# Dividing the exponentials before the transposes, instead of the outputs after the value product

## The chip, the cores and the metric

The kernel runs on one core of a Trainium2 chip. The metric is the device time of one execution in microseconds, as the median of several runs. TensorE (PE) multiplies matrices and also does the transposes; VectorE (DVE), ScalarE (ACT) and GpSimd (POOL) work element by element; SyncE (SP) issues the loads.

## The reference, cut to what matters

Two networks follow each other on 256 tokens of width 1024. The first is a mixer with a mixture of experts. The second has two layers; each normalizes, projects to queries, keys and values, attends, gates the attention's output with silu(z), and projects back. The change lies in the attention of these two layers alone. What it has to compute is, for each head of width 64 with 512 keys (256 of a context, 256 latent):

```
s = q @ k.T * scale (+ mask or position bias)     # layer 0, heads 0-7: one more logit, the sink, in the sum
p = softmax(s, axis=-1)
o = (p @ v) * silu(z)
```

Layer 0 has eight heads with grouped keys and a sink and eight latent-attention heads; layer 1 has sixteen neighbourhood heads with a bias. All is float32.

## The kernel before, in words

The weights stream from memory. Each piece is split into a high part (ACT, tile `whi`) and a rest (`wlo`, DVE, every fourth piece POOL), and each projection is three matmuls per block (`gmm`, line 314). That is most of PE's work.

The attention of a layer is cut into 16 units (`unit`, line 2219): a unit is one pair of heads `c` and one block of 128 queries `i`. `x0_units` makes the units of layer 0 (the first eight with a sink, `sink_softmax`; the last eight with `plain_softmax`), `x1_units` those of layer 1. A unit goes in three parts:

- Scores: for both heads s, scores into a PSUM bank of their own (tag "t", six banks); DVE adds mask or bias and takes the row maximum (`snm`); ACT takes the exponentials into `P` (tile `sP`, three buffers) and their row sums into `sm` (tile `ssm`). DVE turns `sm` into its reciprocal (line 2233), POOL spreads that over 64 columns a head (`rs`, tile `rsb`, line 2234).
- Transposes: `P`, not yet divided, is transposed on PE in eight 128x128 pieces (line 2240 by way of line 433) and evicted to `PT`, the first head by ACT, the second by DVE.
- Values: PE turns `rs` (line 2243) into the first 128 columns of a bank, and multiplies `PT` with the values (line 2246) into the next 128. The first write into the output tile `oz` (tile `xoz`) is ACT's copy of the turned reciprocals, and DVE then multiplies by the values' product; where the gate is there already, DVE multiplies twice instead.

The order on PE is written out in the program: `drive` (line 143) runs all streams (three lanes of units, the projection, the closing steps, small turns) on a clock of its own. A stream that yields `(cost, late)` moves that clock by its cost and may go on only `late` after it; of those that are due, the first in the list goes, and the projection, always due, fills the rest in steps (about 655 clock units for the six matmuls of a step of 256 columns). A unit starts at least `UNIT_GAP` = 3300 after the one before; its transposes follow `UNIT_P` after the scores, its values `UNIT_T` = 1600 after the transposes:

```
yield (900, UNIT_P)      # after the scores
yield (900, UNIT_T)      # after the transposes
yield 1200               # after the values
```

PE, and every other engine, executes its instructions in order. On the other engines a scheduler of the framework sets the order at build time. The context's attention of the first layers (lines 1751 and 1792) already divides its exponentials by `scaled` (line 1861), with 256 keys.

Of the kernel before, what the change touches and what calls it, by code (L numbers as in the profile page):

```python
# [12 lines left out]
OP = mybir.AluOpType  # L13
# [24 lines left out]
POOL_A = 4  # L38
POOL_C = 4
UNIT_GAP = 3300  # L40
UNIT_P = 3000
UNIT_T = 1600
UNIT_Q = 5000
LANES = 3
# [225 lines left out]
class Net:  # L270
# [1948 lines left out]
    def unit(self, c, i, needs, scores, soft, vals):  # L2219

        nc, Y, pm = self.nc, self.Y, self.pm
        mm = nc.tensor.matmul
        yield from self.wait(*needs)
        yield (0, max(0.0, max(self.done.at[n] for n in needs) + UNIT_Q - CLOCK[0]))
        yield ("unit", UNIT_GAP)
        rows = []
        for s in range(2):
            b = self.bank(pm, "t", 6)
            scores(b, s)
            rows.append(b)  # L2230
        P, sm = soft(rows)
        rs = self.t(Y, [128, 128], "rsb", 2)
        nc.vector.reciprocal(sm, sm)
        nc.gpsimd.tensor_copy(rs.rearrange("p (s d) -> p s d", s=2), sm[:, :, None].to_broadcast([128, 2, 64]))
        self.done.add("s%d%d" % (c, i))
        yield (900, UNIT_P)
        PT = self.t(Y, [128, 2, 4, 128], "PT", 2)
        for s in range(2):
            b = self.transposes([(128 * k, P[:, s, 128 * k:128 * k + 128]) for k in range(4)], pm, "t", 6)
            (self.copy if s else self.act)(PT[:, s], b.rearrange("p (k q) -> p k q", k=4))  # L2240
        yield (900, UNIT_T)
        b = self.bank(pm, "t", 6)
        nc.tensor.transpose(b[:, 0:128], rs, self.ident)
        for k in range(4):
            for s in range(2):
                mm(b[64 * s:64 * s + 64, 128:256], vals(k, s), PT[:, s, k], start=False, stop=k == 3,  # L2246
                   skip_group_check=True)
        o = self.oz[:, c, 128 * i:128 * i + 128]
        if "g%d" % (c // 2) in self.done:
            self.tt(o, b[:, 0:128], o, OP.mult)  # L2250
            self.tt(o, b[:, 128:256], o, OP.mult)
        else:
            self.act(o, b[:, 0:128])
            self.tt(o, b[:, 128:256], o, OP.mult)
        self.done.add("o%d%d" % (c, i))
        yield 1200

# [298 lines left out]
```

## Time and profile before

| | us |
|---|---|
| median of 3 runs | 1212.33 (1212.28 to 1212.49) |
| the profiled execution | 1215.19 |
| its span, first to last instruction | 1213.4 |
| busy in the span: PE / DVE / ACT / POOL | 1096.5 / 561.3 / 452.6 / 192.1 |

The profile is of one execution. Busy shares are means over stages with different limits, so a stage is read by itself: the units of layer 0 run from about 895 to 990 us, those of layer 1 from about 1064 to 1170 us. A row of the windows view gives the stretch, its length, and for each engine its busy us and instructions (PEld is the loading of weights on PE), then the granted clock as a share of full speed and the share and GB/s of the DMA engines. In a row of instructions, "tile<-inputs" names what is written and read, and a bracket at its end is the idle time of the engine before it and what ended that.

### The profile page before, as it was taken

The numbers are of one execution on the slowest core, as the hardware profiler recorded it, in microseconds if no ns is written. First come the engines' busy times: TensorE is split into PE (matmuls) and PEld (weight loads), VectorE is DVE, ScalarE is ACT, GpSimd is POOL, SyncE is SP. The second block draws the span as 40 slices with busy tenths as digits, with TensorE's granted clock in tenths as the row PEclk, the third lists the DMA queues.
The fourth block names the chain that finished last, engine by engine and source line by source line (L and its number), as shares of the span: only waits on it lengthen the run. The fifth ranks groups of instructions, "written<-read, shape, count | busy, mean of one in ns | idle before, by whom it ended". The sixth has DMA issues, their size and how long they took to land. (4 is left out here: it accounts for less than half of the span.)

```text
span 1213.4 us, 19686 instructions
## 1 busy us (share of the span) xinstructions
PE 1096.5 (90%) x7695; PEld 759.6 (63%) x7695; DVE 561.3 (46%) x1393; ACT 452.6 (37%) x1107; POOL 192.1 (16%) x210
## 2 busy tenths in 40 slices
PE   5999999998989998788889899957989996999996
PEld 5878777785335664333444265312877786999996
DVE  5366773454131211432311210105797677677776
ACT  4634564541012101222310200004576554676663
POOL 6134102211000000000000000001311143335231
PEclk8999999997999999999999899998999998899999
DMA  7898659972999999999999999997435275355331
GB/s 252 294 303 269 209 168 322 344 286 96 395 407 407 400 403 405 404 405 408 404 402 406 405 405 405 405 400 262 150 105 157 70 145 157 112 142 124 122 111 60
DMA packets 171321, 337.62 MB, mean 278 GB/s; under 512 B 20053, under 2 KB 92826, under 8 KB 171226
## 3 DMA queue, kind: packets, MB, share of 16 engines
q1 hardware_dynamic: 169706, 333.78, 76.5%
q0 software_dynamic: 1104, 2.45, 0.7%
q8 instruction: 62, 1.02, 0.3%
q14 instruction: 33, 0.27, 0.1%
q10 hardware_dynamic: 416, 0.10, 0.1%
HBM read 331.58 MB, written 4.73 MB: 277 GB/s over the span
## 5 line engine op out<-in xcount | busy, mean ns | idle before, releaser
L317 ACT ACTIVATE whi<-wst 128x512 fp32r<-128x512 f32 (+4 forms) x240 | 149.2, 629 | 107.5 <-PE m L314 97.4
L217 DVE TENSOR_TENSOR wlo<-wst,whi 128x512 fp32r<-128x512 f32 (+4 forms) x180 | 137.8, 772 | 82.5 <-ACT whi L317 81.4
L217 POOL TENSOR_TENSOR wlo<-wst,whi 128x512 fp32r<-128x512 f32 (+4 forms) x60 | 80.2, 1337 | 484.6 <-ACT whi L317 407.0
L1390 PE MATMUL g<-we,xg 128*32 128x512 f32 x632 | 127.3, 612 | 11.4 <-DMA we<-in_w_up_dram 9.2
L314 PE MATMUL m<-whi,uhi 128*128 128x256 f32 (+2 forms) x368 | 108.7, 295 | 2.8 <-ACT uhi L317 1.9
L314 PE MATMUL m<-wlo,uhi 128*128 128x256 f32 (+2 forms) x368 | 104.8, 285 | 1.8 <-POOL wlo L217 1.8
L314 PE MATMUL m<-whi,ulo 128*128 128x256 f32 (+2 forms) x368 | 104.7, 285 | 0.0
L314 PE MATMUL s<-cuT,wst 128*128 128x256 f32 (+1 forms) x368 | 85.8, 385 | 0.0
L314 PEld LDWEIGHTS s<-cuT,wst 128*128 128x128 f32 (+1 forms) x368 | 64.7, 183 | 27.6 <-issue 17.1
L314 PEld LDWEIGHTS m<-whi,uhi 128*128 128x128 f32 x368 | 70.5, 192 | 13.0 <-issue 5.8
L314 PE MATMUL m<-xhi,whi 128*128 128x256 f32 x256 | 75.6, 295 | 0.0
L314 PE MATMUL m<-xhi,wlo 128*128 128x256 f32 x256 | 72.4, 283 | 0.0
L314 PE MATMUL m<-xlo,whi 128*128 128x256 f32 x256 | 72.3, 283 | 0.0
L314 PEld LDWEIGHTS m<-wlo,uhi 128*128 128x128 f32 x368 | 70.4, 191 | 2.1 <-POOL wlo L217 2.0
L314 PEld LDWEIGHTS m<-whi,ulo 128*128 128x128 f32 x368 | 70.3, 191 | 0.3 <-POOL ulo L503 0.3
L1421 PE MATMUL d<-we,hT 128*32 128x512 f32 x336 | 59.2, 616 | 6.8 <-DMA we<-in_w_down_dram 6.8
L1390 PEld LDWEIGHTS g<-we,xg 128*32 128x32 f32 x632 | 25.9, 110 | 59.7 <-issue 35.2
L314 PE MATMUL s<-wst,cuT 128*128 128x512 f32 (+1 forms) x160 | 53.7, 480 | 0.0
L314 PEld LDWEIGHTS m<-xhi,whi 128*128 128x128 f32 x256 | 48.9, 191 | 2.7 <-issue 2.5
L314 PEld LDWEIGHTS m<-xlo,whi 128*128 128x128 f32 x256 | 48.9, 191 | 0.7 <-issue 0.5
L314 PEld LDWEIGHTS m<-xhi,wlo 128*128 128x128 f32 x256 | 48.9, 191 | 0.0
L314 PE MATMUL m<-whi,xhi 128*128 128x256 f32 (+2 forms) x144 | 43.2, 300 | 5.2 <-ACT xhi L317 5.0
(611 smaller groups left out, 2303.2 us busy)
## 6 DMA issues: line engine op xcount, KB each, us to landing
we<-in_w_down_dram SPq DMA_DIRECT2D x48, 1024.0 KB
we<-in_w_up_dram SPq DMA_DIRECT2D x40, 1024.0 KB
we<-in_w_gate_dram SPq DMA_DIRECT2D x39, 1024.0 KB
we<-in_ada_w_dram SPq DMA_DIRECT2D x24, 1024.0 KB
wst<-in_c_in_w_dram SPq DMA_DIRECT2D x24, 1024.0 KB
wst<-in_w_in_dram SPq DMA_DIRECT2D x17, 1024.0 KB
wst<-in_ab_in_w_dram SPq DMA_DIRECT2D x16, 1024.0 KB
vc<-in_w_gate_dram SPq DMA_DIRECT2D x12, 1024.0 KB
```

The source lines that it names most:

```text
L217: (net.nc.gpsimd if pool else net.nc.vector).tensor_tensor(b, src, a, OP.subtract)
L314: mm(out, l, r, start=first and i == 0, stop=last and i == len(ps) - 1, skip_group_check=True)
L317: return self.nc.scalar.activation(out, in_, f, **kw)
L1390: nc.tensor.matmul(b[32 * e:32 * e + 32, :], xg[:, 2 * j + r, 32 * e:32 * e + 32], v[e // 2][:, e % 2, 512 * r:512 * r + 512], start=j == ...
L1421: nc.tensor.matmul(ds[hf][32 * e:32 * e + 32, :], hT[:, k, 32 * e:32 * e + 32], v[e // 2][:, e % 2, 512 * hf:512 * hf + 512], start=k == 0 ...
```

## The change

`P` is divided where it lies, by DVE, one instruction a head, ahead of the transposes; the spreading of the reciprocals, their transpose on PE and the second multiplication into `oz` go; the values' product starts its bank by itself. `UNIT_P` goes from 3000 to 4000.

```diff
-UNIT_P = 3000
+UNIT_P = 4000
...
         P, sm = soft(rows)
-        rs = self.t(Y, [128, 128], "rsb", 2)
         nc.vector.reciprocal(sm, sm)
-        nc.gpsimd.tensor_copy(rs.rearrange("p (s d) -> p s d", s=2), sm[:, :, None].to_broadcast([128, 2, 64]))
+        for s in range(2):
+            self.ts(P[:, s], P[:, s], sm[:, s:s + 1])
...
         b = self.bank(pm, "t", 6)
-        nc.tensor.transpose(b[:, 0:128], rs, self.ident)
         for k in range(4):
             for s in range(2):
-                mm(b[64 * s:64 * s + 64, 128:256], vals(k, s), PT[:, s, k], start=False, stop=k == 3,
+                mm(b[64 * s:64 * s + 64, 0:128], vals(k, s), PT[:, s, k], start=k == 0, stop=k == 3,
                    skip_group_check=True)
         o = self.oz[:, c, 128 * i:128 * i + 128]
         if "g%d" % (c // 2) in self.done:
             self.tt(o, b[:, 0:128], o, OP.mult)
-            self.tt(o, b[:, 128:256], o, OP.mult)
         else:
             self.act(o, b[:, 0:128])
-            self.tt(o, b[:, 128:256], o, OP.mult)
```

`self.ts(out, a, s)` is DVE's tensor_scalar: each row of `a` times that row's scalar `s`.

## Rows read from the trace of the kernel before

**Rows 1.** Windows: busy us of PE, PEld, DVE, ACT, POOL; clock; DMA.
```profile
895.00:915.00 20.00, 17.68 (x130) 14.91 (x129) 19.57 (x87) 14.07 (x39) 2.77 (x4) 1.00 0.50 143
945.00:990.00 45.00, 45.00 (x369) 36.39 (x367) 30.80 (x60) 25.82 (x62) 10.03 (x14) 1.00 0.35 95
1064.00:1080.00 16.00, 16.00 (x141) 14.31 (x141) 13.56 (x31) 12.73 (x30) 5.88 (x7) 1.00 0.49 148
```

**Rows 2.** PE's waits, 1064 to 1170 us: us in total, times, longest.
```profile
PE t L2246 <- DVE PT L331: 1.0, 2, 0.6
```

**Rows 3.** The chain of waits: start us, us, engine, line; here only PE.
```profile
1072.59 0.11 PE t L2243
1072.69 1.02 PE t L2246 x16
...
1074.74 0.72 PE m L314 x6
```

**Rows 4.** Groups of what goes: min/median/max ns, or busy us, mean ns.
```profile
L2243 PE MATMUL t<-tab,rsb x32: 270/272/328, 906.2 to 1167.7; 128*128 128x128 f32 x32
L2234 POOL COPY rsb<-ssm x32: 287/294/611, 902.7 to 1164.4; 128x128 f32<-128x128 f32 x32
...
L320 DVE TENSOR_TENSOR xoz<-t,xoz 128x128 f32<-128x128 f32 x32 | 9.2, 287 | 7.3 <-ACT xoz L317 7.0
```

**Rows 5.** The timeline of PE around one such transpose: start us, us.
```profile
1072.42 0.27 PE L2243 MATMUL t<-tab,rsb 128*128 128x128 f32 x1
1072.62 0.66 PE L2246 MATMUL t<-PT,vc 128*64 128x128 f32 x8
```

**Rows 6.** Tensor_scalar on DVE: the group of line 327, then timeline rows.
```profile
L327 DVE TENSOR_SCALAR sP<-sP,ssm x32: 344/351/354, 475.9 to 605.5; 128x256 f32<-128x256 f32 x32
...
475.75 0.17 DVE L1862 RECIPROCAL ssm<-ssm 128x2 f32<-128x2 f32 x1
475.95 0.62 DVE L327 TENSOR_SCALAR sP<-sP,ssm 128x256 f32<-128x256 f32 x2
...
685.94 1.41 DVE L327 TENSOR_SCALAR cxa<-cuT,rcy 128x1024 f32<-128x1024 f32 x2
```

**Rows 7.** The timeline at the third unit of each four in layer 1.
```profile
1074.96 0.28 DVE L320 TENSOR_TENSOR xoz<-t,xoz 128x128 f32<-128x128 f32 x1
1075.16 0.68 DVE L331 COPY PT<-t 128x512 f32<-128x512 f32 x1
...
1076.22 0.49 PE L433 MATMUL t<-tab,sP 128*128 128x128 f32 x3
1076.31 0.17 DVE L2233 RECIPROCAL ssm<-ssm 128x2 f32<-128x2 f32 x1 [0.47 <-ACT sP L317]
...
1099.28 1.04 PE L433 MATMUL t<-tab,sP 128*128 128x128 f32 x8
1099.65 0.17 DVE L2233 RECIPROCAL ssm<-ssm 128x2 f32<-128x2 f32 x1 [0.49 <-ACT sP L317]
...
1130.77 0.93 PE L433 MATMUL t<-tab,sP 128*128 128x128 f32 x7
1131.08 0.17 DVE L2233 RECIPROCAL ssm<-ssm 128x2 f32<-128x2 f32 x1 [0.42 <-ACT sP L317]
...
1160.29 0.93 PE L433 MATMUL t<-tab,sP 128*128 128x128 f32 x7
1160.38 0.17 DVE L2233 RECIPROCAL ssm<-ssm 128x2 f32<-128x2 f32 x1 [0.42 <-ACT sP L317]
```

**Rows 8.** The timeline at a unit of layer 0 with a sink.
```profile
915.71 1.32 PE L433 MATMUL t<-tab,sP 128*128 128x128 f32 x8 [0.98 <-ACT sP L317]
...
916.45 0.16 DVE L320 TENSOR_TENSOR ssm<-ssm,ssk 128x2 f32<-128x2 f32 x1 [0.34 <-ACT ssk L317]
```

**Rows 9.** The timeline of DVE and POOL, 874 to 877 us.
```profile
874.28 2.33 DVE L327 TENSOR_SCALAR xqb<-xqb,rs4y 128x384 f32<-128x384 f32 x4
...
875.20 1.26 POOL L217 TENSOR_TENSOR wlo<-wst,whi 128x512 fp32r<-128x512 f32 x1 [3.50 <-ACT whi L317]
```

## The prediction

> **What bounds the kernel now.** Begin with the windows of the two stretches in which units run, since the shares of the whole span mix them with other stages. From 945 us on PE is busy for every microsecond of the stretch, and again in layer 1; the granted clock is 1.00 there [rows 1]. PE's waits say the same: in the 106 us of layer 1's units it loses 1.0 us, on an eviction by DVE [rows 2]. The head of layer 0 is different: between 895 and 915 us DVE is busy for 19.57 of 20 us and PE for 17.68 [rows 1]. So PE's work is the time of most units, DVE's at the head of layer 0, and DVE stands close behind PE where layer 1's units are dense (13.56 of 16 us).
>
> Then look at where a unit's reciprocal lies against its transposes, in the timeline. PE begins the transposes as soon as the exponentials are there; in the third unit of each four of layer 1 the reciprocal starts only after that, by 0.09, 0.37, 0.31 and 0.09 us [rows 7]. Now that costs nothing, for nobody needs the reciprocal until the values' product. The change puts it, and two more instructions, ahead of the transposes.
>
> **What goes.** On PE 32 transposes of the spread reciprocals. In the chain of waits, which follows end to end, one takes 0.11 us [rows 3], so 32 x 0.11 = 3.5 us. From its start to the start of the product behind it are 0.20 us [rows 5], but that holds the product's own beginning; 32 x 0.20 = 6.4 us is the upper end. I take 3.5, since PE is the bound nearly wherever they stand. On DVE one multiplication a unit, 0.287 us long [rows 4], with 0.20 us from its start to the next instruction's [rows 7]. POOL's spreading (0.294 us, [rows 4]) gates the product alone and is no PE wait in layer 1 [rows 2]: nothing for the path.
>
> **What comes.** Two tensor_scalars of 128x512 a unit. No row has that width. One of 256 columns takes 0.351 us; two take 0.62, so the second starts 0.27 after the first; two of 1024 columns take 1.41 [rows 6]. A pair of 512 by proportion: 0.62 + (1.41 - 0.62)/3 = 0.88, one 0.48, start to start 0.40. The bounds for a unit are 0.62 and 1.41; I take 0.88, with 0.80 of DVE's time, net 0.60 after the multiplication that goes. From the start of the reciprocal to a divided first head are 0.20 [rows 6] + 0.48 = 0.68 us, some 0.70 with the hop to PE. The second head (0.20 + 0.88) is needed four transposes later and isn't what decides.
>
> **What moves.** `UNIT_P` puts the transposes 1000 clock units later. What that is in PE work has to be followed through the planner, for the projection comes in steps of about 655. At 3000, the first unit of four (scores at clock 0, cost 900) is due at 3900, behind the second unit's scores, which end at 4424: it goes at once. At 4000 it is due at 4900: one step goes ahead, then it. The other three also gain one step, not one and a half. A step is six matmuls, 0.72 us [rows 3]. The transposes take their evictions, the product and the write into `oz` along; no load is issued in these parts. The exponentials' three buffers serve three lanes with one unit each, so the longer hold delays no one. Steps that come forward by 0.72 us need their weights that much earlier; PE has no wait on a split in these stretches now [rows 2], so I take nothing for it, with 1 us for both layers as the upper end.
>
> **The sum for layer 1.** Take the third unit of the first four [rows 7]. PE would begin its transposes at 1076.22 + 0.72 - 0.11 (one reciprocals' transpose less ahead of it) = 1076.83. The reciprocal comes later, because DVE is in order and full: the two units ahead put 2 x 0.80 in front of it, one multiplication of 0.20 goes, and 0.47 us of idle time ahead of it take up a part: 0.93 later, at 1077.24. Divided at 1077.24 + 0.70 = 1077.94: PE waits 1.11 us. In the same way 0.37 + 0.91 + 0.70 - 0.61 = 1.37, then 0.31 + 0.98 + 0.09 = 1.38 and 0.09 + 0.98 + 0.09 = 1.16 for the other three [rows 7]; together 5.0 us. A wait of PE moves the units behind it along too, so one for each four is counted, at its third unit. Behind the waiting transposes PE's queue holds projection steps, the product of the unit before and the scores of the next, all of them on the path. The lower end is 0 (DVE's order, set anew, has the divisions in time); the upper, with pairs of 1.41 us, about 3 x 0.5 us more for each four, is 11.
>
> **The sum for layer 0.** At the head DVE is full and PE waits for it [rows 1]. Three units have their reciprocal before 915 us: 3 x 0.60 = 1.8 us. A sink's unit needs one more hop: the sum with the sink is ready at 916.61, so the divided head could be there at about 917.3, while its transposes begin at 915.71 [rows 8]: 1.6 us late, less a step of 0.72, 0.9. The later units with a sink have projection work beside them: 0.3 for all. Together 3.0; 0 is the lower end (work put off past 915 us), 5 the upper, with 0.9 for two more. From 945 to 990 us DVE is busy for 30.8 of 45 us [rows 1] and takes up 8 x 0.60 = 4.8 more: nothing.
>
> Sum: -3.5 + 5.0 + 3.0 = +4.5 us. On the profiled execution, 1215.19 us (span 1213.4 and 1.8 around it), that is 1219.7; the median of the runs is 2.9 below that execution, so 1216.8.
>
> **A rule against the change.** Four tensor_scalars (two of 384, two of 256 columns) took 2.33 us, where the pairs above would give about 1.3, and a POOL split of 1.26 us began among them [rows 9]. The Trainium skill (SBUF — State Buffer, "Who interferes with whom") says that VectorE in a two-port mode, which a float32 tensor_scalar within SBUF can enter, and GpSimd take turns on one port pair, the second waiting for the whole instruction of the first; by that rule, the trace agrees, these divisions would queue behind POOL's splits. As a mechanism of these rows: in layer 1's first four POOL is busy for 5.88 of 16 us, 4.7 without the four spreadings, so a tensor_scalar meets one with a chance of 0.29 and waits half of 1.26 us, 0.18 in the mean; five of them ahead of the third unit's transposes make 0.9 us for each four, 3.7 in layer 1.
>
> **Rivals.**
> *The cover is enough* (chance 0.20): the divisions are in time, the saving is left: 1215.19 - 3.5 - 2.9 = 1208.8. It ends on the other side, by one mechanism: at the third unit of each four, DVE has the reciprocal 1.1 to 1.4 us earlier than I reckon, because its order, set anew, puts weight splits behind the divisions. For it: the idle time ahead of each reciprocal in rows 7. Against: DVE's 13.56 of 16 us [rows 1], and that full DVE at 895 to 915 us would have to take 1.8 us more for nothing.
> *Gain and wait cancel* (0.25): only the head of layer 0 pays in full, and a tenth of layer 1's waits come: -3.5 + 3.0 + 0.5 = 0, 1212.3. For it: layer 1's DVE has 2.4 us of idle time in those 16 us [rows 1], and the head of layer 0 none.
> *Divisions behind POOL* (0.13): the mechanism of rows 9 on top of the forecast, +8.2 us: 1220.5. It decides once a third of the divisions meet POOL. Against: POOL loses 32 instructions, and some divisions will be first.
> *Forecast* (0.42): 1216.8, by itself 1214.8 to 1219.
>
> **The numbers.** About 0.2% (2.4 us) is what a measurement of this kernel tells from no change. Slower by more: forecast and POOL, 0.42 + 0.13 = 0.55; within: 0.25; faster: 0.20. The range goes from the full saving, 1208.8, past the POOL case to 1221.0; below it lies a saving of 0.20 a transpose, above it pairs of 1.41 us, together about one in ten, and as much again for what I haven't seen.
>
> **What would show it.** Right: PE's waits in layer 1 name the tensor_scalar (line 327) ahead of transposes (line 433), about 1.2 us at each four, mostly at third units; DVE in 1064 to 1080 goes from 13.6 to over 15 us; between 895 and 915 us PE's busy time falls. The removed transposes shorten PE's work by 3.5 us in all. Wrong: no such waits in layer 1 (then the time is at or under 1212), transposes moved by other than one step, a tensor_scalar far from 0.48 us, or waits in other stretches.

## The result, and the profile after

| | us |
|---|---|
| before, median of 5 runs | 1212.49 (1212.28 to 1215.32) |
| after, median of 5 runs | 1230.71 (1228.41 to 1235.15) |
| ratio after/before, 95% interval | 1.0143 (1.0127 to 1.0160) |
| the profiled execution of after, and its span | 1235.15, 1233.4 |

The change made the kernel slower by 1.43%, some 17 us. The sign was forecast; the size was not. The forecast was +4.5 us, and 1230.71 lies above the range.

Where the time went is found by cutting both executions at the same work, not at the same microsecond: from the first scores of layer 0 to its first out-projection matmul (the units of layer 0), from there to the first scores of layer 1 (call it the seam), from there to the first out-projection matmul of layer 1 (its units). The windows view gives one row for each of the three; its columns are those of [rows 1]. First the kernel before:

```profile
895.60:990.08 94.48, 91.42 (x729) 73.93 (x729) 68.34 (x195) 59.06 (x151) 18.99 (x27) 1.00 0.42 117
990.08:1064.47 74.39, 63.22 (x452) 60.27 (x451) 53.93 (x120) 40.30 (x94) 29.43 (x23) 0.89 0.58 151
1064.47:1179.86 115.39, 114.38 (x995) 104.88 (x993) 83.98 (x163) 76.34 (x168) 40.93 (x48) 1.00 0.46 121
```

The same three stretches of the kernel after:

```profile
897.41:997.40 99.99, 91.00 (x714) 72.79 (x713) 77.76 (x209) 60.11 (x151) 15.94 (x12) 0.98 0.43 114
997.40:1070.59 73.19, 63.02 (x452) 60.42 (x451) 55.12 (x123) 40.62 (x94) 27.85 (x22) 0.88 0.54 149
1070.59:1199.76 129.17, 116.76 (x978) 105.40 (x977) 98.79 (x179) 76.59 (x168) 36.10 (x32) 0.99 0.39 108
```

The profiled executions differ by 19.96 us (1235.15 - 1215.19). The units of layer 0 take 5.5 of it, those of layer 1 13.8, the seam gives 1.2 back, and 1.9 lie elsewhere: 1.8 of it ahead of layer 0's units, in work that the change leaves as it is (the first scores begin at 895.60 and 897.41 us here, and between 893.2 and 898.7 in the profiles of the experiments). In layer 1 PE was idle for 1.01 us before (115.39 - 114.38) and is for 12.41 after. PE's waits say for what; us in total, times, longest. The units of layer 0, before and, below the dots, after:

```profile
PE t L433 <- DVE qp L320: 2.1, 2, 1.6
PE t L433 <- ACT sP L317: 1.0, 1, 1.0
...
PE t L433 <- DVE sP L327: 6.4, 6, 1.9
PE t L433 <- DVE qp L320: 2.0, 2, 1.6
PE t L433 <- ACT whi L317: 0.6, 1, 0.6
```

The units of layer 1 after, against the single row of [rows 2] before:

```profile
PE t L433 <- DVE sP L327: 9.0, 9, 2.6
PE t L2245 <- DVE PT L331: 3.3, 4, 1.2
```

The wait on the division (line 327, ahead of the transposes of line 433) is there by name as forecast, 15 times and not four or five, and a second one has grown behind it: the values' product waiting for DVE's eviction of `PT`, 3.3 us where it was 1.0. Together they grew by 11.3 us, of layer 1's 13.8.

The division itself has the size that was reckoned. The group of line 327, min/median/max in ns:

```profile
L327 DVE TENSOR_SCALAR sP<-sP,ssm x64: 470/481/2110, 904.4 to 1184.0; 128x512 f32<-128x512 f32 x64
```

The forecast was 0.48 for one and 0.88 for a pair, and both are what the rows show but for five stretched pairs of the 32 (see POOL's part). At the longest wait the pair took its 0.88 us, so a slow instruction is not what made it. What it is shows best in the rows around it, the timeline at the third unit of the second four of layer 1 (rows of DVE, ACT and PE; start us, us):

```profile
1107.65 1.28 DVE L1853 TENSOR_REDUCE snm<-t 128x1 f32<-128x512 f32 x2
...
1108.29 0.63 ACT L317 ACTIVATE whi<-wst 128x512 fp32r<-128x512 f32 x1 [0.43 <-PE m L314]
...
1108.83 0.67 ACT L317 ACTIVATE sP<-t,snm 128x512 f32<-128x512 f32 x1
1108.85 0.68 DVE L217 TENSOR_TENSOR wlo<-wst,whi 128x512 fp32r<-128x512 f32 x1
1109.44 0.69 DVE L331 COPY PT<-t 128x512 f32<-128x512 f32 x1
1109.49 0.68 ACT L317 ACTIVATE sP<-t,snm 128x512 f32<-128x512 f32 x1
...
1110.29 0.17 DVE L2232 RECIPROCAL ssm<-ssm 128x2 f32<-128x2 f32 x1 [0.16 <-ACT sP L317]
1110.38 0.67 DVE L217 TENSOR_TENSOR wlo<-wst,whi 128x512 fp32r<-128x512 f32 x1
1110.96 0.88 DVE L327 TENSOR_SCALAR sP<-sP,ssm 128x512 f32<-128x512 f32 x2
1111.59 1.42 PE L433 MATMUL t<-tab,sP 128*128 128x128 f32 x8 [2.56 <-DVE sP L327]
...
1112.94 1.12 PE L2245 MATMUL t<-PT,vc 128*64 128x128 f32 x8
```

Read it from the bottom up. The transposes waited 2.56 us for the division. The division began 0.67 us after the reciprocal and not 0.20, because DVE's order has a weight split (`wlo`) between the two. The reciprocal itself waited for the exponentials. ACT began those at 1108.83, in line behind its own part of a weight split (`whi`, from 1108.29), some 0.5 us after DVE had the first of the two row maxima (line 1853; two reductions, 1107.65 to 1108.93). The way of a unit to its transposes thus leads three times through DVE, for the maxima, the reciprocal and the division, with ACT in between, and each step stands in its engine's order. In numbers: the reciprocal started 1.26 us after the transposes could have (1111.59 - 2.56 = 1109.03), where the prediction's figures give 0.67, and the first head was there 1.30 us after the reciprocal's start, where 0.70 was reckoned.

In 18 of the 32 units another instruction stands between reciprocal and division, 0.27 to 0.73 us from start to start; in the others it is 0.20.

### The profile page after: what moved, and what is told of

It is laid out like the page before. It is cut to its first block, busy times and chain, and to the rows that moved or that the text cites. A ratio compares the mean times of both kernels' runs of the same rounds, so it can differ in the third digit from the quotient of the medians.

```text
span 1233.4 us, 19594 instructions
## 1 busy us (share of the span) xinstructions
PE 1099.7 (89%) x7663; PEld 761.0 (62%) x7663; DVE 587.3 (48%) x1425; ACT 454.3 (37%) x1107; POOL 182.5 (15%) x178
## 4 chain that ended last, share of the span: by engine, by line
PE 46%; DVE 12%; DMA 10%; ACT 5%; issue 2%; POOL 1%; SPq 0%; ACTq 0%; DVEq 0%; POOLq 0%
PE s L314 11%; PE m L314 10%; PE g L1390 7%; DMA we<-in_w_down_dram 5%; PE d L1421 3%; PE t L433 3%; PE t L2245 2%; DVE wlo L217 2%; ACT sP L317 2%; PE t L1292 2%; DMA we<-in_w_up_dram 2%; DMA we<-in_w_gate_dram 1%; DVE sP L327 1%; DVE h L320 1%; PE t L2275 1%
## 5 line engine op out<-in xcount | busy, mean ns | idle before, releaser
L433 PE MATMUL t<-tab,sP 128*128 128x128 f32 x256 | 36.1, 282 | 16.1 <-DVE sP L327 15.3
```

The source lines that it names most:

```text
L433: self.nc.tensor.transpose(b[:s.shape[1], o:o + 128], s, self.ident)
```

## The experiments

All ratios are against runs of the kernel before on the same chip, with their 95% intervals. "Cost" below is a ratio of two ratios, in us of about 1214; its interval takes the two as independent.

**The later place alone.** The kernel before, with the change's `UNIT_P`.

```diff
-UNIT_P = 3000
+UNIT_P = 4000
```

> The kernel before with UNIT_P at 4000, nothing divided early. Theory A (PE's transposes wait for the divisions, which stand in a full DVE queue): within 3 us of before, 1209 to 1215, and no wait of PE on tile sP. Rival B (the later place of the transposes on PE costs by itself, through the products and evictions behind them): 1220 or more, with the waits on PT (3.3 us in layer 1 after the change) here too.

Measured: 0.9969 (0.9955 to 0.9983). The later place alone gains 3.8 us. In the profile the units of layer 0 took 92.46 us against 94.48, the seam 70.51 against 74.39, with the granted clock at 0.93 there instead of 0.89; layer 1 is unchanged (115.95). No wait of PE names `sP`, so the later place costs nothing by itself, and the rival's 1220 is out. The true price of the division is thus to be read against this kernel: 1.0143/0.9969 = 1.0175, 21 us (18.5 to 24).

**The division without the later place.** The change, with the old `UNIT_P`.

```diff
-UNIT_P = 4000
+UNIT_P = 3000
```

> The change with UNIT_P left at 3000. Theory A: slower than the change, since 0.72 us of cover is gone at each unit: waits on sP of 25 us or so in place of 15.3, 1234 to 1242. Rival B: back near before, 1209 to 1216.

Measured: 1.0205 (1.0182 to 1.0228), 24.8 us over before, as was expected. The waits on the division are 16.9 us in 16 places, well short of the 25 that were expected with it. The later place of the change is worth 0.0062, 7.5 us (4 to 11).

**The load without the wait.** The change, but the divided exponentials go into a tile that nobody reads; DVE does nearly the same amount of work (173.2 us in the two stretches of units, 176.6 in the change), and the transposes read the undivided ones.

```diff
+        aside = self.t(Y, [128, 512], "aside", dt=mybir.dt.bfloat16)
         for s in range(2):
-            self.ts(P[:, s], P[:, s], sm[:, s:s + 1])
+            self.ts(aside, P[:, s], sm[:, s:s + 1])
```

> The change, but the divided exponentials go to a tile that nobody reads (bf16, one head wide, for lack of room), and the transposes take the undivided ones; the outputs are thus not normalized. DVE's load is that of the change, PE waits for no division. Theory A: the 15 us of waits on sP are gone and the 3.5 us of transposes stay saved: 1209 to 1216. Rival C (DVE's load is what costs, through score additions, evictions and weight splits that come late, whoever waits for the division): 1222 to 1230, with PE waiting on PT, wlo or the exponentials instead.

Measured: 1.0058 (1.0039 to 1.0076), between the two expectations. The profiled execution is the fastest of its eight (1216.07 us, median 1220.73), so its rows rather understate the loss. Its waits of PE in the units of layer 1, and the stretch:

```profile
PE t L2246 <- DVE PT L331: 7.7, 8, 1.5
PE t L433 <- ACT sP L317: 0.6, 1, 0.6
```

```profile
1056.90:1180.74 123.84, 115.51 (x979) 104.85 (x977) 97.60 (x179) 76.88 (x168) 36.16 (x32) 1.00 0.42 113
```

Nothing waits for a division, and layer 1 is 8.5 us longer than before all the same. The values' product waits for `PT`, and this eviction is late because DVE is. (An undisturbed pair takes 1.01 us here and not 0.88, since its second instruction starts 0.52 us after the first and not 0.40; the load is thus not quite that of the change.)

**The wait without the load.** The change, but each division is of one column of 512.

```diff
-            self.ts(P[:, s], P[:, s], sm[:, s:s + 1])
+            self.ts(P[:, s, 0:1], P[:, s, 0:1], sm[:, s:s + 1])
```

> The change, but each division takes only the first column of a head's exponentials (the other columns stay undivided): PE still waits for reciprocal and division, DVE has 0.15 us an instruction in place of 0.48. Theory A, where wait and load are needed together: the wait is shorter than the 0.72 us of cover, 1209 to 1216. Rival D (the place of the reciprocal behind other work on DVE is enough, whatever the division takes): 1220 to 1228, with waits on sP of 8 us or more.

Measured: 1.0023 (1.0006 to 1.0040). The time is within the first expectation (to 1216 us, 1.003), the waits are the 8 us of the rival. PE's waits in the two stretches of units, layer 0 and layer 1, in this order:

```profile
PE t L433 <- DVE sP L327: 3.7, 5, 1.5
...
PE t L433 <- DVE sP L327: 4.4, 6, 0.8
PE t L2245 <- DVE PT L331: 0.7, 1, 0.7
```

The hop through DVE costs 8.1 us of waits even when the instruction in it takes 0.20 us and not 0.48. It is not quite a wait without a load: DVE is busy for 154.0 us in the two stretches, 10.5 more than in the next run, which divides nothing (143.55); the change adds 33.0 to that.

**Neither.** The change without the two divisions: the base for the two above, and the test of what the removed instructions gave.

```diff
-        for s in range(2):
-            self.ts(P[:, s], P[:, s], sm[:, s:s + 1])
```

> The change without its two divisions (the outputs are not normalized; the reciprocal is still taken): neither DVE's load nor PE's wait, only the saving, with UNIT_P at 4000. It is the base from which load alone (e3_divide_aside), wait alone (e4_wait_small) and both (the change) are counted. Theory A2 (load and wait both cost, and the saving is real): e1_late_only less 3.5 us, ratio to before 0.991 to 0.996. Rival (the transposes on PE were hidden and save nothing): as e1_late_only, 0.997.

Measured: 0.9961 (0.9947 to 0.9975). The windows of its units of layer 0 and of layer 1:

```profile
898.01:988.95 90.94, 88.60 (x713) 71.69 (x713) 63.53 (x177) 58.94 (x151) 15.67 (x12) 1.00 0.46 125
...
1059.99:1174.52 114.53, 113.24 (x979) 103.94 (x977) 80.02 (x147) 75.60 (x168) 35.56 (x32) 1.00 0.46 122
```

From this base the load alone costs 0.0097 (11.8 us), the wait alone 0.0062 (7.5 us), and both together, the change, 0.0182 (22 us). They add up to 19.3; each interval is about 2.6 us wide to either side, so the sum and the whole agree. The parts are not cleanly apart: the run of the wait alone holds about a third of the load (10.5 of 33.0 us on DVE), so its 7.5 us are an upper end for the hop. The stretches of units say nearly the same, 11.1 and 8.1 us over this base against 23.7 for the change; the lower clock, 3.4 us in the change and in neither of the two (see below), makes most of that difference. Neither alone explains the result. Against the first experiment, whose units took 92.46 and 115.95 us, this one's are 1.52 and 1.42 us shorter, 2.9 for the 32 transposes and the multiplications that are gone; the timed ratios (0.9961 and 0.9969) can't tell 1 us from 3, nor the expectation from its rival.

**The load on another engine.** ACT divides.

```diff
-            self.ts(P[:, s], P[:, s], sm[:, s:s + 1])
+            self.act(P[:, s], P[:, s], AF.Copy, scale=sm[:, s:s + 1])
```

> The change with the divisions on ACT (activation Copy with a scale by row) in place of DVE. DVE's load is gone, a division of about 0.63 us stands in ACT's queue, and none shares a port with POOL. Theory A2 (DVE's load, by late evictions, is about half of the loss): ratio 1.000 to 1.008, with waits on sP by ACT. Rival D2 (any full queue does it; ACT has 12.7 of 16 us busy in layer 1's first four before, and 5 more come): 1.012 or more, with waits on whatever ACT evicts.

Measured: 1.0044 (1.0029 to 1.0058). The wait on the division is there still, 8.7 us in 11 places, now on ACT; the wait on `PT` falls to 0.4 us. It behaves like the wait alone; the 0.0021 between them are within the noise (0.0022). ACT, 35 us busier in the two stretches than in the change, carried the load that DVE could not; the hop stays on ACT too.

**More cover.** The change, and the kernel before, each with `UNIT_P` at 6000.

```diff
-UNIT_P = 4000
+UNIT_P = 6000
```

> The change with UNIT_P at 6000, some two projection steps more of cover. Theory A2: the waits on sP go from 15 us to under 5, the load of DVE stays, as in e3_divide_aside: ratio 1.002 to 1.008. Rival E (the waits follow DVE, not the planner's place; with lanes as long as this the units draw apart and end later): 1.012 or more.

> The kernel before with UNIT_P at 6000, nothing divided early. If what e1_late_only gained came from transposes that no longer wait for exponentials or the eviction behind them, more distance gives as much or a little more: ratio 0.994 to 0.998. If it came from a changed order at the seam of the two layers alone, it can go either way: 0.995 to 1.005, with the seam (layer 0's last products to layer 1's first scores) longer or shorter by 3 us or more.

Measured: 1.0008 (0.9990 to 1.0025) with the divisions, 0.9955 (0.9939 to 0.9972) without. The cost of the division is 1.0008/0.9955, 6.5 us (3.5 to 9.4), where it was 21 at 4000 and 24.8 at 3000: the waits on the division fall to 3.6 us in 4 places. The run with the divisions is faster than was expected (1.002 to 1.008): the whole is less than what the load alone cost at 4000 (11.8), so cover helps against the load too. Cover cures most of the change, but not all, and the kernel that doesn't divide early profits from the same cover.

**POOL's part.** Some of DVE's time is stretching. The 32 pairs of divisions took 33.3 us, 5.1 more than 32 x 0.88. In the units of after, DVE instructions that lasted over 1.25 times the median of their kind (line, tiles and shape) make 16.7 us more than that median; without the divisions it is 7.9 us, not the 6.3 of the expectation below. The largest, with the POOL instruction beside it (timeline of after):

```profile
938.14 2.50 DVE L327 TENSOR_SCALAR sP<-sP,ssm 128x512 f32<-128x512 f32 x2
...
938.41 1.95 POOL L2372 MEMSET kA<- 128x2048 f32 x1 [4.25 <-PE t L2265]
```

And one that reaches PE, by way of a weight split and not of a division:

```profile
1078.60 1.29 POOL L217 TENSOR_TENSOR wlo<-wst,whi 128x512 fp32r<-128x512 f32 x1 [7.23 <-ACT whi L317]
1078.73 1.71 DVE L217 TENSOR_TENSOR wlo<-wst,whi 128x512 fp32r<-128x512 f32 x1
...
1080.36 0.68 DVE L331 COPY PT<-t 128x512 f32<-128x512 f32 x1
...
1081.09 0.54 PE L2245 MATMUL t<-PT,vc 128*64 128x128 f32 x5 [1.19 <-DVE PT L331]
```

A split of 0.69 us took 1.71 beside POOL's, the eviction behind it came 1 us late, and PE waited 1.19 us. To size this, all weight splits from layer 0 on went to DVE (26; 17 of them in the two stretches of units, where the expectation counts 18), in the change and in the kernel before with `UNIT_P` at 4000:

```diff
-POOL_C = 4
+POOL_C = 0
```

> The change, with every weight split from layer 0 on given to DVE (none of every fourth to POOL). In the two stretches of units that takes 18 splits of 1.3 to 1.4 us from POOL and gives DVE 18 more of 0.69 us, 12.4 us of work. Question: which part of the change's cost (1.0143 against 0.9969 with UNIT_P alone, 1.75% or 21 us) comes from DVE instructions stretched by a POOL instruction beside them. They make 16.6 us of DVE's time in these stretches with the change and 6.3 us without the divisions. Theory of full DVE (the divisions' length on DVE and the wait for them; POOL's lock an addition): DVE is fuller, the cost is as large or larger, ratio 1.014 or more, 21 us or more over its control. Rival, POOL's lock: the stretched pairs go with the splits, the cost falls to two thirds or less, 14 us or less over its control.

> Control of the run with the divisions and no splits on POOL: the kernel before with UNIT_P at 4000 and every weight split from layer 0 on given to DVE. With UNIT_P alone the ratio was 0.9969 and PE waited 1.0 us in layer 1's units; DVE takes 17 more splits of 0.69 us there and loses some stretched ones. Both theories: within 0.3% of 0.9969, since DVE has 30% of idle time in the units there; above 1.000 would say that DVE bounds the units already without the divisions.

Measured: 1.0071 (1.0055 to 1.0087) with the divisions, 0.9930 (0.9915 to 0.9945) without. The stretching fell from 16.7 us to 6.2. The cost of the division is 1.0071/0.9930 = 1.0142, 17 us (14.5 to 20), against 21 (18.5 to 24): POOL's splits have a share of 4 us, within 3.8 either way, and neither of the two expectations (14 or less, 21 or more) was met; the run without divisions is a little faster than was expected of it (within 0.3% of 0.9969). PE's waits in the units of layer 0 and, below the dots, of layer 1 of the kernel that divides:

```profile
PE t L433 <- DVE sP L327: 4.0, 5, 1.2
...
PE t L433 <- DVE sP L327: 9.5, 7, 2.6
PE t L2245 <- DVE PT L331: 0.8, 2, 0.6
```

In layer 1 the waits on the division are as they were (9.0); most of the waits on `PT` have gone (3.3 before), although DVE is as busy as it was (100.60 us of 126.55). So the late evictions of after came for a good part from stretched instructions ahead of them and not from DVE's fullness as such. In layer 0 the waits on the division did fall, from 6.4 us to 4.0, and the clock stayed at 1.00. Each against its kernel without divisions, the profiles have 3.8 us less in layer 0's units and 1.0 less in layer 1's. The order on DVE is another one in these two runs as well, so not all of that need be stretching. The load alone was run with POOL's splits in place, so its 11.8 us hold some of it; what the load costs without them was not run. And the stretched sum is no measure of the cost, for it is 10.2 us in the change at `UNIT_P` 3000, which costs most, and 17.5 at 6000, which costs least. The run with neither divisions nor POOL's splits, 1204.99 us, is the fastest of all: it beats both kernels, by 0.7% and by 2.1%.

## Why the prediction was right in sign and wrong in size

**The removed transposes (-3.5): right.** PE's busy time in the two stretches is 88.60 and 113.24 us without them against 90.18 and 114.88 in the first experiment, 3.2 us less, and the stretches are 2.9 us shorter.

**The division's length (0.48, 0.88 a pair): right** for 27 of 32 pairs, as the group of line 327 shows.

**One planner step of cover, 0.72 us: right for layer 1, wrong for layer 0.** Count the projection's matmuls on PE between the last scores of a unit and its transposes, before and after. In layer 1 it is six more in 14 of the 16 units and twelve more in the other two. Of the eight units with a sink, where layer 0's waits are, only three gained any (the fourth and the sixth twelve, the seventh six); three of the five waits there stand at units that gained none. **"No wait from 945 to 990 us": nearly right.** The window of [rows 1] after:

```profile
945.00:990.00 45.00, 44.27 (x361) 33.78 (x358) 32.95 (x70) 25.32 (x63) 6.26 (x5) 1.00 0.26 68
```

PE lost 0.7 us there. **The signs: right, at the same work.** The units of layer 0 and of layer 1 began 1.8 and 6.1 us later than before. Over the first 16 us of layer 1's units DVE was busy for 15.12 us, against 13.6 of 16 before [rows 1] (over 15 was forecast), and over the 20 us at the head of layer 0 PE was busy for 16.29 (896.81 to 916.81 us), against 17.68:

```profile
1070.59:1086.59 16.00, 13.86 (x106) 12.35 (x104) 15.12 (x32) 10.86 (x24) 2.07 (x2) 1.00 0.43 132
```

**The sum for layer 1 (+5.0): this is the step that failed.** "A wait of PE moves the units behind it along too, so one for each four is counted, at its third unit." The third units waited 0.95, 2.56, 0.97 and 1.33 us, 5.8 in all, where 1.11, 1.37, 1.38 and 1.16 were reckoned: that part holds in sum. But five more waits stand at other units, 3.2 us, and 2.3 us were added at `PT`. What was wrong in it:

- The other units were left out, on the ground that a wait moves them along. Each of their five waits has a cause of its own. The first unit of the third four waited 0.89 us; in the kernel before its reciprocal already trailed its transposes by 0.28 us, like those of the third units (rows below the list). Two more (0.60 us at 1090.41, 0.68 at 1176.65) stand behind a weight split between reciprocal and division, 0.69 and 0.67 us from start to start. The last two (0.78 at 1091.82, 0.20 at 1121.83) are waits for a second head whose division was stretched beside POOL. With the hop and little load (the wait alone) there are six waits in layer 1 already.
- The delay was reckoned from the reciprocals' place alone. At the longest wait (2.56 instead of 1.37) the exponentials ahead of the reciprocal were late as well, and a split went between reciprocal and division: 0.67 us from start to start where 0.20 was taken.
- The 0.60 us of DVE's time a unit were set against DVE's idle time, and the evictions of `PT` were not priced. The load alone costs 11.8 us over both layers (in the profiles 9.3 in layer 1's units and 1.8 in layer 0's). DVE's busy time rose by 24.2 us in the two stretches (77.76 + 98.79 - 68.34 - 83.98), 0.76 a unit; the 0.16 above the forecast are the divisions' stretching: the 32 pairs took 33.3 us and not 32 x 0.88 = 28.2.

In the timeline of before, the first unit of the third four:

```profile
1123.60 1.03 PE L433 MATMUL t<-tab,sP 128*128 128x128 f32 x8
...
1123.88 0.16 DVE L2233 RECIPROCAL ssm<-ssm 128x2 f32<-128x2 f32 x1
```

**The sum for layer 0 (+3.0): low by half.** Of the 6.4 us of waits on the division, 6.2 come ahead of 945 us, in five places, at units with a sink. The mechanism was the one given for the sink's unit, one hop more; "the later units with a sink have projection work beside them: 0.3 for all" was not so. The trace of before spoke against it: the reciprocals of the fifth, sixth and eighth unit started 0.48, 1.60 and 0.92 us after their transposes, and at the unit of [rows 8] the reciprocal started 1.07 us after the sum (ready at 916.61) from which the prediction went on:

```profile
917.68 0.15 DVE L2233 RECIPROCAL ssm<-ssm 128x2 f32<-128x2 f32 x1
```

And the step of cover that was to help was not there for most of these units.

**`UNIT_P` by itself: priced at nothing, worth -3.8 us.** It has hidden a part of the cost: without it the change would have been 24.8 us slower.

**The clock: not priced.** It is granted below 1.00 in two stretches of units where it was 1.00 before, behind the wait of 1.93 us that ended at 924.14, and in the 3.4 us from 1111.6 us on, behind the wait of 2.56 us:

```profile
924.42:927.83 3.41, 3.41 (x25) 2.75 (x23) 1.26 (x2) 0.65 (x2) 0.00 (x0) 0.50 0.87 229
...
1111.60:1115.00 3.40, 3.40 (x25) 2.74 (x25) 0.93 (x2) 0.64 (x2) 0.00 (x0) 0.58 0.00 0
```

That is the lower of the two levels, 1.2 of 2.4 GHz (in the second row for the most part), after an idle PE. Eight values' products took 1.12 us there; eight like them took 0.66 at 1086.79, as in [rows 5]. Each of the two stretches is 3.4 us long, so it lost about half of that, 1.7 us; together 3.4 us. That the waits brought them is argued from the order in time: both came within 0.6 us behind the two longest waits. It is no rule, for in the run without POOL's splits a wait of 2.56 us that ended at 1101.78 was followed by a clock of 1.00.

**The rivals.** *The cover is enough* and *gain and wait cancel* are out at `UNIT_P` 4000; the second came about at 6000 (1.0008). *Divisions behind POOL*: the mechanism is there. The Trainium skill (SBUF — State Buffer, "Who interferes with whom") has VectorE and GpSimd take turns on one port pair, and the stretched rows agree: all five stretched divisions end 0.28 or 0.29 us after the POOL instruction beside them. Its price, 3.7 us, is near the 4 that the last two runs give, but by luck. It was reckoned for the third units of layer 1, where no stretched division made PE wait more than 0.14 us; what the profiles show is 1.0 us in layer 1, partly by stretched splits ahead of the evictions, and 3.8 in layer 0. Of 32 pairs of divisions only five lasted over 1.2 us.

**What adds up.** In layer 1's units the waits on the division (9.0 us), the growth of the wait on `PT` (2.3) and the clock (1.7), less the transposes (1.4), make 11.6 of 13.8 us; in layer 0's, new waits of 6.4 and 0.6, less the one of 1.0 that went, 6.0 + 1.7 - 1.5 = 6.2 where 5.5 were found. What stays open: some 2 us of layer 1, which lie inside PE's busy time (116.76 us; the base without divisions has 113.24, and the clock adds 1.7), as they do with the load alone (115.51 at a clock of 1.00); and whether and how `UNIT_P` shortens the seam. Without the divisions it went from 74.39 us at 3000 to 70.51 at 4000 and 67.93 at 6000, with a higher granted clock each time, but these are single executions, and the other profiles at 4000 have seams of 68.9 to 73.2 us.

## What to carry to other kernels

Putting an operation between a producer and the engine that bounds the kernel can cost twice: the hop, even if the instruction is short (up to 7.5 us here), and the load, on everything else which that engine owes the bound one (11.8 us here, through evictions above all). Work both out for every unit, not for the worst of each group: the old trace shows how far each unit's result lies behind the place where it will be needed, and what the order on the engine puts between. When a change comes with a new constant that hides it, give the constant to the old kernel as well before judging: here it was worth 3.8 us by itself, and more of it (0.9955), or the same with POOL's splits given to DVE (0.9930), beat both kernels.

## What was unexpected of the hardware

Five divisions on DVE that began beside a POOL instruction (from 0.02 us before its start to 0.24 after) lasted 0.85 to 2.11 us where 0.48 is the median, and each ended 0.28 or 0.29 us after that instruction, whatever its length (0.60 to 1.95 us). In four other runs, the division without the later place, the load alone, the change at `UNIT_P` 6000 and the change without POOL's splits, 24 more divisions over 0.6 us end at the same distance. Divisions that a POOL instruction joined later, by 0.15 to 0.42 us, kept their 0.48. Weight splits on DVE (0.69 us) were stretched as well, up to 1.82 us. Moving 26 splits of mostly 1.3 to 1.4 us from POOL to DVE, 17 of them in the two stretches of units (11.7 us more work for the fuller engine), made the kernel before with `UNIT_P` at 4000 faster, 0.9930 against 0.9969, and left DVE no busier in the units of the kernel that divides (77.76 and 98.79 us with POOL's splits, 76.59 and 100.60 without).
